# A trunk layer on one core: separate places for raw weights, low parts by adding DMAs at the channel mixer's front, and the last gate computed there

## The chip, the cores and the metric

The kernel runs on one core of a Trainium2 chip. The metric is the device time of one execution in microseconds, the median over several executions. The names of the engines are those of the profile: PE is TensorE, DVE VectorE, ACT ScalarE, POOL GpSimd, SP SyncE.

## The reference

One layer on a sequence of 512 rows of width 1024, in float32: a token mixer (attention and a diagonal state-space branch on one modulated input, merged by gates) and a SwiGLU channel mixer, each modulated by a conditioning vector through shift, scale and gate.

```python
mod = c_act @ w_ada[l] + b_ada[l]
sh_m, sc_m, g_m, sh_f, sc_f, g_f = [m[:, None, :] for m in jnp.split(mod, N_MOD, axis=-1)]
h = _normalize(x) * (1.0 + sc_m) + sh_m
y = token_mixer(h, ...)
x = _layer_norm(DEEPNORM_ALPHA * x + (1.0 + g_m) * y, ln1_g[l], ln1_b[l])
h = _normalize(x) * (1.0 + sc_f) + sh_f
gate, up = jnp.split(h @ w_ffn_in, 2, axis=-1)
y = (jax.nn.silu(gate) * up) @ w_ffn_out
x = _layer_norm(DEEPNORM_ALPHA * x + (1.0 + g_f) * y, ln2_g[l], ln2_b[l])
```

`w_in` has 4096 columns (q, k, v, the state-space input u and two gates of 1024), `w_ffn_in` 2 x 2816, `w_ada` 6 x 1024.

## The kernel before

Every large product runs on PE in three matmuls on rounded operands (`mm3`): high times high, high times low, low times high. So each weight tile of 128x1024 passes four steps: SP loads it into a raw place, ACT casts it to its high part `whi` (L178, L1054), and the low part `wlo` is raw minus high. `unit` has two ways for the low part: a subtraction on DVE or POOL (`sub`, recorded as L159), or, with `eng=None`, ACT writes minus raw (L180) and a DMA from POOL's queue adds raw to it (L181). `whi` and `wlo` have four places each (`NHI`); `slot_unit` and `split` put such parts into the 53 general slots `s0` to `s52` instead.

**Raw places.** All raw data rotate through eight places of one tag, "raw" (`NRAW`): weights, the raw blocks of `w_ada` (`ra`), and the coefficient tables `ce` of the state-space slices (L598 to L601, two for a slice, alive from the memset on POOL to the slice's last matmul). The ninth tile of the tag waits until the first is free, the tenth for the second, whatever they hold. SP issues its loads in program order (`load`, L146), so a load that waits for its place holds back all loads behind it.

**Token mixer.** Four state-space slices (`ssm_slice`) alternate with eight dense tiles of `w_in`: six for q and k (`qk_tile`) and two for v (`v_tiles`, 256 columns, two raw pieces of 512 KB each). The gates of the conditioning vector for the token mixer and the vectors of the channel mixer's modulation are summed on DVE from `ra` blocks (`ada_acc`, L250 and L252) while gate tiles, attention and the up-projections run. Then follow the output projection (`proj`) and, block by block of 128 rows, the first layer norm (`ln1_block`, L934 to L984), which transposes on PE (L967), modulates on DVE and ACT (L972, L974) and writes high and low parts of the channel mixer's input `h` (L978, L159).

**Channel mixer, front.** Four first weights of `w_ffn_in` (two by `unit`, two by `slot_unit`; the subtraction on POOL, POOL, POOL and DVE by `FENG`), then `first_half(0)`, which multiplies them with the first 256 rows; then for the first two of ten column groups `p_x1` (product `X`) and `p_b`, each of one raw piece (`piece`) whose low part DVE subtracts in `operand` (L1054 and L159); then `first_half(256)` and `combine`.

**Channel mixer, loop.** For each of the ten groups `dp` seven products on raw pieces and their sums (`plus`, L1047). In groups 2 to 5 the loop also computes a quarter of the last gate `g_f` on PE (`ada_gate_pe`, L259 to L273: a memset on POOL, L264, one small load of `b_ada`, two loads of `w_ada` of 512 KB, 16 matmul records of 128x32 by 32x256), and in group 6 two products with `ones` spread it over the rows, into the slots `gmx` of the first gate. Then follows the down projection on `w_ffn_out`.

The order of the work on each engine is set by the framework's scheduler from the program's order, its priorities (`prio`) and the pools.

Of the kernel before, what the change touches and what calls it, by code (L numbers as in the profile page):

```python
# [13 lines left out]
F32 = mybir.dt.float32  # L14
F32R = mybir.dt.float32r
I32 = mybir.dt.int32
AF = mybir.ActivationFunctionType
ALU = mybir.AluOpType

P = 128  # L20
# [36 lines left out]
PL = 5  # L57
TAIL = 256

ENG, FENG = "VGVVVGVGGGGVVGGG", "GGGV"  # L60


XE, BE, ME, HE = "VVVV", "VVVV", "VVAVAAAV", "VVVVVVVV"
# [18 lines left out]
def _build(tc, I, out):  # L82
# [6 lines left out]
    def nm(s):  # L89
        cnt[0] += 1  # L90
        return f"{s}_{cnt[0]}"
# [50 lines left out]

    banks = [psp.tile([P, 512], F32, tag=f"b{i}", name=f"b{i}") for i in range(8)]

    def load(o, i):
        return tc.keep_in_program_order(nc.sync.dma_start(out=o, in_=i))  # L146

# [10 lines left out]
    def sub(dst, a, b, eng=V):  # L158
        return eng.tensor_tensor(dst, a, b, ALU.subtract)  # L159

    def split(x, n=512, eng=V, keep=False):

        h, l = get(F32R), get(F32R)
        acopy(h[:, :n], x[:, :n])  # L164
        sub(l[:, :n], x[:, :n], h[:, :n], eng)
        if not keep:
            put(x)
        return h, l

    def unit(view, a, b, eng=V):  # L170


        with prio("feed"):
            raw = wp.tile([P, D], F32, tag="raw", name=nm("raw"), bufs=NRAW)
            load(raw.rearrange("p (a b) -> p a b", a=a), view)
            hi = wp.tile([P, D], F32R, tag="whi", name=nm("whi"), bufs=NHI)
            lo = wp.tile([P, D], F32R, tag="wlo", name=nm("wlo"), bufs=NHI)
            acopy(hi, raw)  # L178
            if eng is None:
                act(lo, raw, AF.Copy, scale=-1.0)  # L180
                G.dma_start(out=lo, in_=raw, accum_op=ALU.add)  # L181
            else:
                sub(lo, raw, hi, eng)
        return hi.rearrange("p (a b) -> p a b", a=a), lo.rearrange("p (a b) -> p a b", a=a)

    def slot_unit(view, a, b, eng=V):

        raw = wp.tile([P, D], F32, tag="raw", name=nm("raw"), bufs=NRAW)
        load(raw.rearrange("p (a b) -> p a b", a=a), view)
        return [split(raw[:, h * 512:(h + 1) * 512], 512, eng, keep=True) for h in range(2)]  # L190

# [49 lines left out]
    def ada_acc(dst, src, n, init=None):  # L241

        m = D // n
        for k in range(KC):
            if k % m == 0:
                raw = wp.tile([P, D], F32, tag="raw", name=nm("ra"), bufs=NRAW).rearrange("p (k n) -> p k n", k=m)
                load(raw, src[:, k:k + m, :])
            r_ = raw[:, k % m, :]
            if k == 0 and init is None:
                ts(dst, r_, ca[:, 0:1], None, ALU.mult)  # L250
            else:
                stt(dst, r_, ca[:, k:k + 1], init if k == 0 else dst, ALU.mult, ALU.add)  # L252
# [8 lines left out]
    def ada_gate_pe(j, i, dst):  # L261

        col = j * D + i * 256
        G.memset(dst, 0.0)  # L264
        load(dst[0:1, :], I["b_ada"][0:1, col:col + 256])
        o = bk.get()
        for k0 in (0, 4):
            raw = wp.tile([P, D], F32, tag="raw", name=nm("ra"), bufs=NRAW).rearrange("p (k n) -> p k n", k=4)
            load(raw, w_ada[:, k0:k0 + 4, col:col + 256])
            for g in range(4):  # L270
                mm(o[32 * g:32 * g + 32, 0:256], caz[:, k0 + g, :], raw[:, g, :], k0 == 0, k0 == 4, tile_position=(0, 32 * g))
        tt(dst, o[:, 0:256], dst, ALU.add)
        bk.put(o)  # L273

# [291 lines left out]
    def ssm_slice(s):  # L566
# [29 lines left out]
        shc = [P, 4, 5, 16]  # L596
        ce = []
        for i in range(2):  # L598
            x_ = wp.tile([P, D], F32, tag="raw", name=nm("ce"), bufs=NRAW)[:, 0:640]
            G.memset(x_, 0.0)  # L600
            ce.append(x_.rearrange("p (q l g c) -> p q l g c", q=4, l=5, g=2))  # L601
        l5 = [bc(x[:, q4, 0:5], shc, [3]) for x in (lre, lim, nre, nim)]
# [109 lines left out]
    for s in range(4):  # L712
        with prio("ssm"):
            ys.append(ssm_slice(s))
        with prio("qkv"):
            for f in dense[2 * s:2 * s + 2]:
                f()
    put(spar_, *sbc_, *spp)


    HALVES = [(0, [(384, [(0, 0, 256), (1, 256, 128)])]),
# [181 lines left out]
    with prio("mix"):  # L903
# [92 lines left out]
        for i in range(NT):  # L996
            with prio("first"):
                ln1_block(i)
        put(*l1g, *l1b)


    with prio("ffn"):
        first, wx = [], []
        for i in range(FIRST):
            for c in (0, FH):
                view = w_f[:, :, c + P * i:c + P * i + P]
                if len(first) < 2:
                    w = unit(view, KC, P, (V, G)[FENG[len(first)] == "G"])
                    w = [[x[:, k, :] for x in w] for k in range(KC)]
                else:  # L1010
                    pair = slot_unit(view, KC, P, (V, G)[FENG[len(first)] == "G"])
                    wx += pair
                    w = [[x[:, k % 4 * P:k % 4 * P + P] for x in pair[k // 4]] for k in range(KC)]
                first.append(w)
        part = [get() for _ in range(FIRST)]

        def first_half(n0):
            ts_ = slice(n0, n0 + 256)
# [17 lines left out]

        def piece(dp, c, k0):
            with prio("feed"):
                raw = wp.tile([P, D], F32, tag="raw", name=nm("raw"), bufs=NRAW)
                col = c + P * (FIRST + 2 * dp)  # L1040
                load(raw.rearrange("p (a b) -> p a b", a=4), w_f[:, k0:k0 + 4, col:col + 256])
            return raw

        def plus(x, y):
            with prio("feed"):
                r = wp.tile([P, D], F32, tag="raw", name=nm("raw"), bufs=NRAW)
                tt(r, x, y, ALU.add)  # L1047
            return r

        def operand(x):  # L1050
            with prio("feed"):
                hi = wp.tile([P, D], F32R, tag="whi", name=nm("whi"), bufs=NHI)
                lo = wp.tile([P, D], F32R, tag="wlo", name=nm("wlo"), bufs=NHI)
                acopy(hi, x)  # L1054
                sub(lo, x, hi)
            return hi, lo

        def product(o, x, h, first):
            w = operand(x)
            for q in range(2):  # L1060
                for k in range(4):
                    cs = slice(k * 256 + q * P, k * 256 + q * P + P)
                    mm3(o[:, q * 256:q * 256 + 256], [x_[:, cs] for x_ in w], h[k], first and q == 0 and k == 0, k == 3)
# [39 lines left out]
        def p_x1(dp):  # L1103
            d = dps[dp]
            d["a"], d["c"] = piece(dp, 0, 0), None
            d["X"], d["c1"] = bk.get(), get()
            product(d["X"], d["a"], half(0, 0), True)
            acopy(d["c1"], d["X"])

        def p_b(dp):  # L1110
            d = dps[dp]
            d["b"] = piece(dp, 0, 4)
            o = bk.get()
            product(o, d["b"], half(4, 0), True)
            tt(d["c1"], o, d["c1"], ALU.add)
            bk.put(o)
            silu(d["c1"])

        first_half(0)
        for dp in range(2):  # L1120
            p_x1(dp)
# [4 lines left out]
        for x in wx:  # L1126
            put(*x)
        acts, spent = [], []
        gfx = gmx
        for g in part:  # L1130
            h_ = split(g)
            acts.append(lambda m, h_=h_: [x[:, m * P:(m + 1) * P] for x in h_])
# [1 line left out]
        for dp in range(ND):  # L1134
            d, nxt = dps[dp], 2 <= dp + 1 < ND
            c_, d_ = piece(dp, FH, 0), piece(dp, FH, 4)
            s1 = plus(c_, d_)
            s2 = plus(s1, d["a"])
            product(d["X"], s2, hM, False)
            v = get()  # L1140
            acopy(v, d["X"])
            y = bk.get()
            product(y, s1, hN, True)
            product(d["X"], plus(d["a"], c_), hB, False)
            w = get()
            acopy(w, d["X"])
            tt(w, y, w, ALU.add)
            if nxt:
                p_x1(dp + 1)
            product(d["X"], d_, hD, False)  # L1150
            stt(d["c1"], d["X"], -1.0, d["c1"], ALU.mult, ALU.mult)
            bk.put(d["X"])
            if nxt:
                p_b(dp + 1)
            product(y, plus(s2, d["b"]), half(4, 256), False)
            tt(v, y, v, ALU.add)
            bk.put(y)
            silu(v)
            stt(v, w, -1.0, v, ALU.mult, ALU.mult)
            put(w)  # L1160
            d["f"] = d["c1"], v
            if 2 <= dp < 6:
                j = dp - 2
                ada_gate_pe(5, j, gfx[j // 2][:, j % 2 * 256:j % 2 * 256 + 256])
            if dp == 6:
                for j in range(2):
                    p_ = bk.get()
                    mm(p_, ones, gfx[j], True, True)
                    act(gfx[j], p_, AF.Identity, bias=one_c)
                    bk.put(p_)  # L1170
        put(*held)
        def parts(dp):

# [5 lines left out]
        with after(silus[-1:]):  # L1179
            for m in range(NT):  # L1180
                for h in range(2):
                    act(x1[m][h], x1[m][h], AF.Copy, scale=ALPHA)
        pf = [[bk.get(), bk.get()] for i in range(NT)]
        for kc in range(NF - LAST):
            if kc == len(acts):
# [107 lines left out]
```

## Time and profile before

| | |
|---|---|
| median of 3 executions | 824.61 us (824.35 to 826.85) |
| the profiled execution | 824.6 us |
| its span, first to last instruction | 822.9 us |
| granted TensorE clock, mean over the span | 0.968 of full speed |
| DMA | 111.49 MB, 135 GB/s on average |

The span is the time between the first and the last instruction of the trace; 1.7 us of the execution lie outside it. Times on the trace count from the start of the span. PEclk is the clock granted to TensorE as a share of 2.4 GHz; half of it is 1.2 GHz. A row of a timeline gives start, duration, engine, line, operation, output<-input, and in brackets how long the engine was idle before it and what ended that.

### The profile page before, as it was taken

The page shows a single profiled execution, that of the slowest core. Times are in us where ns is not written, and L with a number is a line of the kernel's source. Part 1 is how long each engine was busy: PE and PEld are TensorE (multiplying, and loading weights), DVE is VectorE, ACT ScalarE, POOL GpSimd, SP SyncE. Part 2 cuts the span into 40 slices and gives each one's busy share as a digit, 9 for nine tenths or more (in the row PEclk, how much of TensorE's full clock was granted, in tenths as well). Part 3 has the DMA queues.
Part 4 walks back from the last instruction along what each step waited for, and adds up shares of the span by engine and source line. Part 5 has one row for each costly group of instructions (what it writes and reads, how often), then busy time and mean ns, then how long its engine had stood idle before and what let it go on. Part 6 is the DMA issues. An engine that isn't in the chain of part 4 may idle for free.

```text
span 822.9 us, 12321 instructions
## 1 busy us (share of the span) xinstructions
PE 758.1 (92%) x4767; PEld 667.5 (81%) x4767; DVE 586.4 (71%) x975; ACT 438.8 (53%) x715; POOL 148.4 (18%) x161
## 2 busy tenths in 40 slices
PE   4989989999996797999994999999999999999995
PEld 2878879988885676787883989999999999888884
DVE  5798474884658774878799898777787876434267
ACT  4375644678987676761435473534445456532211
POOL 1443244512323221001634000000000000000013
PEclk9999998999997999899998899999999999999998
DMA  9992227964207792925941004414445344440001
GB/s 281 361 242 67 52 64 153 237 137 77 52 10 196 228 232 92 350 70 187 358 120 52 1 19 136 155 53 146 144 143 183 104 139 145 157 148 27 1 26 76
DMA packets 99498, 111.49 MB, mean 135 GB/s; under 512 B 4456, under 2 KB 86384, under 8 KB 99440
## 3 DMA queue, kind: packets, MB, share of 16 engines
q1 hardware_dynamic: 95552, 96.82, 37.1%
q0 software_dynamic: 3744, 13.63, 9.0%
q8 instruction: 37, 0.61, 0.3%
q10 hardware_dynamic: 144, 0.26, 0.1%
q14 instruction: 21, 0.17, 0.1%
HBM read 94.97 MB, written 2.10 MB: 118 GB/s over the span
## 4 chain that ended last, share of the span: by engine, by line
PE 75%; DVE 10%; DMA 6%; issue 3%; ACT 2%; SPq 2%; POOL 1%; POOLq 0%; DVEq 0%; ACTq 0%
PE b L149 74%; DMA ra<-w_ada 3%; SPq L146 2%; DMA s<-w_in 1%; DVE s L252 1%; DVE st L288 1%; DMA raw<-w_glu 1%; DMA wlo<-raw 1%; DVE h L159 1%; DVE s L407 1%; DMA s<-x 0%; DVE s L159 0%; DVE s L972 0%; DVE s L943 0%; DVE s L477 0%
## 5 line engine op out<-in xcount | busy, mean ns | idle before, releaser
L149 PE MATMUL b<-h,whi 128*128 128x256 f32 (+1 forms) x896 | 216.5, 331 | 20.8 <-DVE h L159 9.4
L149 PEld LDWEIGHTS b<-h,whi 128*128 128x128 f32 x896 | 151.5, 191 | 36.5 <-DVE h L159 9.6
L159 DVE TENSOR_TENSOR wlo<-raw,whi 128x1024 fp32r<-128x1024 f32 x103 | 129.6, 1264 | 72.1 <-ACT whi L178 37.1
L149 PE MATMUL b<-s,whi 128*128 128x256 f32 (+1 forms) x800 | 168.5, 308 | 7.6 <-ACT whi L178 6.8
L149 PE MATMUL b<-h,wlo 128*128 128x256 f32 (+1 forms) x448 | 148.2, 331 | 1.4 <-DMA wlo<-raw 1.4
L149 PEld LDWEIGHTS b<-s,whi 128*128 128x128 f32 x800 | 129.7, 190 | 18.0 <-ACT whi L178 6.9
L149 PE MATMUL b<-whi,s 128*128 128x512 f32 (+1 forms) x392 | 122.6, 390 | 0.0
L149 PE MATMUL b<-s,wlo 128*128 128x256 f32 (+1 forms) x400 | 121.5, 306 | 0.0
L159 DVE TENSOR_TENSOR s<-s,s 128x512 fp32r<-128x512 f32 (+4 forms) x112 | 76.4, 689 | 56.4 <-PE b L149 23.0
L178 ACT CAST whi<-raw 128x1024 fp32r<-128x1024 f32 x66 | 69.0, 1048 | 84.7 <-PE b L149 66.5
L1054 ACT CAST whi<-raw 128x1024 fp32r<-128x1024 f32 x70 | 72.7, 1050 | 77.5 <-PE b L149 41.6
L149 PEld LDWEIGHTS b<-h,wlo 128*128 128x128 f32 x448 | 85.8, 192 | 8.9 <-DMA wlo<-raw 1.9
L149 PEld LDWEIGHTS b<-whi,s 128*128 128x128 f32 x392 | 73.2, 188 | 16.6
L149 PE MATMUL b<-s,s 128*128 128x128 f32 (+2 forms) x438 | 81.9, 317 | 2.0 <-POOL s L159 1.4
L164 ACT CAST s<-s 128x512 fp32r<-128x512 f32 (+1 forms) x106 | 57.7, 569 | 41.3 <-DMA s<-w_in 12.1
L149 PEld LDWEIGHTS b<-s,wlo 128*128 128x128 f32 x400 | 75.7, 190 | 3.7
L149 PEld LDWEIGHTS b<-s,s 128*128 128x128 f32 x438 | 68.5, 192 | 11.2 <-POOL s L159 1.6
L149 PE MATMUL b<-wlo,s 128*128 128x512 f32 (+1 forms) x196 | 76.4, 390 | 0.0
L1233 POOL TENSOR_TENSOR s<-s,s 128x512 f32<-128x512 f32 x6 | 8.5, 1430 | 357.1 <-DVE s L1232 357.1
L159 POOL TENSOR_TENSOR s<-s,s 128x512 fp32r<-128x512 f32 (+1 forms) x32 | 40.2, 1264 | 79.0 <-ACT s L164 77.6
L1047 DVE TENSOR_TENSOR raw<-raw,raw 128x1024 f32<-128x1024 f32 x40 | 48.6, 1219 | 4.8 <-DMA raw<-w_ffn_in 4.3
L252 DVE SCALAR_TENSOR_TENSOR s<-ra,ca,s 128x256 f32<-128x256 f32 x88 | 47.2, 557 | 4.0 <-DMA ra<-w_ada 3.2
(246 smaller groups left out, 1096.1 us busy)
## 6 DMA issues: line engine op xcount, KB each, us to landing
raw<-w_ffn_in SPq DMA_DIRECT2D x44, 512.0 KB, 4.5
ra<-w_ada SPq DMA_DIRECT2D x32, 512.0 KB, 7.2
raw<-w_in SPq DMA_DIRECT2D x26, 512.0 KB, 4.7
wlo<-raw POOLq DMA_DIRECT2D x26, 512.0 KB, 5.2
raw<-w_ffn_out SPq DMA_DIRECT2D x22, 512.0 KB, 3.3
wa<-w_ada SPq DMA_DIRECT2D x12, 512.0 KB, 7.6
raw<-w_out SPq DMA_DIRECT2D x12, 512.0 KB, 6.5
s<-x SPq DMA_DIRECT2D x16, 256.0 KB, 3.4
```

The costliest lines, as they stand in the source:

```text
L146: return tc.keep_in_program_order(nc.sync.dma_start(out=o, in_=i))
L149: return nc.tensor.matmul(o, lhsT, rhs, start=start, stop=stop, skip_group_check=True, **kw)
L159: return eng.tensor_tensor(dst, a, b, ALU.subtract)
L164: acopy(h[:, :n], x[:, :n])
L178: acopy(hi, raw)
L252: stt(dst, r_, ca[:, k:k + 1], init if k == 0 else dst, ALU.mult, ALU.add)
L288: V.bn_stats(st[:, i, :], x)
L407: e.scalar_tensor_tensor(p_, n, -c, p_, ALU.mult, ALU.add)
L1047: tt(r, x, y, ALU.add)
L1054: acopy(hi, x)
L1233: G.tensor_tensor(z[h], z[h], l2b[h], ALU.add)
```

## The change

Three parts, and what the scheduler makes of them.

- **Places.** The eight raw places get names, `raw0` to `raw7`. Weights rotate through 0 to 3, `ra` blocks through 4 and 5, `ce` tables through 6 and 7; after the last slice 6 and 7 join the weights. From the channel mixer's pieces on, a list of free places takes the place of rotation: 4, 5, then the weights' six; `raw_get` takes the first free one, `raw_put` gives it back after the last use.
- **Low parts by DMA.** `lower` holds both ways of making a low part. With `eng=None` the four first weights and the four products `p_x1` and `p_b` of groups 0 and 1 now take ACT and a DMA from POOL's queue. That is ten more negations on ACT (six of 128x1024, four of 128x512) and ten more adding DMAs; two subtractions of 128x1024 and two of 128x512 leave POOL, four of 128x1024 and two of 128x512 leave DVE.
- **The last gate.** The four `ada_gate_pe` and the two products with `ones` move from the loop to a place ahead of `first_half(0)`, into two new slots instead of `gmx`.

```diff
+    pieces_of = {"w": deque(range(4)), "ra": deque([4, 5]), "ce": deque([6, 7])}
+
+    def piece_of(kind, name):
+
+        i = pieces_of[kind][0]
+        pieces_of[kind].rotate(-1)
+        return wp.tile([P, D], F32, tag=f"raw{i}", name=nm(name), bufs=1)
+
+    held_raw = {}
+
+    def raw_get():
+
+        i = raws.popleft()
+        x = wp.tile([P, D], F32, tag=f"raw{i}", name=nm("raw"), bufs=1)
+        held_raw[id(x)] = i, x
+        return x
+
+    def raw_put(*xs):
+        for x in xs:
+            raws.append(held_raw.pop(id(x))[0])
...
+    def lower(l, x, h, eng):
+
+        if eng is None:
+            act(l, x, AF.Copy, scale=-1.0)
+            G.dma_start(out=l, in_=x, accum_op=ALU.add)
+        else:
+            sub(l, x, h, eng)
...
     def unit(view, a, b, eng=V):
...
-            raw = wp.tile([P, D], F32, tag="raw", name=nm("raw"), bufs=NRAW)
+            raw = piece_of("w", "raw")
...
             if k % m == 0:
-                raw = wp.tile([P, D], F32, tag="raw", name=nm("ra"), bufs=NRAW).rearrange("p (k n) -> p k n", k=m)
+                raw = piece_of("ra", "ra").rearrange("p (k n) -> p k n", k=m)
                 load(raw, src[:, k:k + m, :])
...
         for i in range(2):
-            x_ = wp.tile([P, D], F32, tag="raw", name=nm("ce"), bufs=NRAW)[:, 0:640]
+            x_ = piece_of("ce", "ce")[:, 0:640]
             G.memset(x_, 0.0)
...
     put(spar_, *sbc_, *spp)
+    pieces_of["w"].extend([6, 7])
...
-                    w = unit(view, KC, P, (V, G)[FENG[len(first)] == "G"])
+                    w = unit(view, KC, P, None)
...
-                    pair = slot_unit(view, KC, P, (V, G)[FENG[len(first)] == "G"])
+                    pair = slot_unit(view, KC, P, None)
...
         part = [get() for _ in range(FIRST)]
+        raws = deque([4, 5, *pieces_of["w"]])
...
-            product(d["X"], d["a"], half(0, 0), True)
+            product(d["X"], d["a"], half(0, 0), True, None if dp < 2 else V)
...
-            product(o, d["b"], half(4, 0), True)
+            product(o, d["b"], half(4, 0), True, None if dp < 2 else V)
...
+        gfx = [get(), get()]
+        for j in range(4):
+            ada_gate_pe(5, j, gfx[j // 2][:, j % 2 * 256:j % 2 * 256 + 256])
+        for j in range(2):
+            p_ = bk.get()
+            mm(p_, ones, gfx[j], True, True)
+            act(gfx[j], p_, AF.Identity, bias=one_c)
+            bk.put(p_)
         first_half(0)
...
-        gfx = gmx
...
-            product(d["X"], plus(d["a"], c_), hB, False)
+            raw_put(s1)
+            s3 = plus(d["a"], c_)
+            raw_put(d["a"], c_)
+            product(d["X"], s3, hB, False)
+            raw_put(s3)
...
-            if 2 <= dp < 6:
-                j = dp - 2
-                ada_gate_pe(5, j, gfx[j // 2][:, j % 2 * 256:j % 2 * 256 + 256])
```

In the order of the instructions two places change. **At the v tiles** (`v_tiles`, raw_260 and raw_263 with whi_261 and whi_264 are the two pieces of the first; ce_179 and ce_180 the tables of the second slice, ce_243 and ce_244 of the fourth), POOL before:

```order
L563 TENSOR_TENSOR ce_179_1098<-s4_181_1102,s6_182_1103 64x20x16
L560 TENSOR_TENSOR s44_183_1108<-s0_101_666,s10_11_86 128x320
L561 TENSOR_TENSOR s7_184_1109<-s0_101_666,s10_11_86 128x320
L562 TENSOR_TENSOR ce_180_1100<-s44_183_1108,s7_184_1109 64x20x16
L563 TENSOR_TENSOR ce_180_1100<-s44_183_1108,s7_184_1109 64x20x16
L574 MEMSET s14_202_1247 128x512
L574 MEMSET s15_203_1248 128x512
L181 DMA wlo_262_1552<-raw_260_1549 128x1024
L181 DMA wlo_265_1559<-raw_263_1556 128x1024
```

and with the change:

```order
L186 DMA wlo_233_1401<-raw_231_1398 128x1024
L186 DMA wlo_262_1552<-raw_260_1549 128x1024
L645 MEMSET s34_187_1126 128x512
L186 DMA wlo_265_1559<-raw_263_1556 128x1024
L586 TENSOR_TENSOR s4_181_1102<-s41_100_665,s10_11_86 128x320
L587 TENSOR_TENSOR s6_182_1103<-s41_100_665,s10_11_86 128x320
L186 DMA wlo_268_1666<-raw_266_1663 128x1024
L626 MEMSET ce_179_1098 128x640
L586 TENSOR_TENSOR s44_183_1108<-s0_101_666,s10_11_86 128x320
L626 MEMSET ce_180_1100 128x640
L587 TENSOR_TENSOR s7_184_1109<-s0_101_666,s10_11_86 128x320
L588 TENSOR_TENSOR ce_179_1098<-s4_181_1102,s6_182_1103 64x20x16
```

The adding DMAs of the v pieces (L186 now) have moved ahead of the second slice's tables, and the memsets of these tables (L626), which stood far ahead, stand right before their products. PE there, before:

```order
L149 MATMUL b4_70<-ce_179_1098,s23_185_1114 128x128
L149 MATMUL b4_70<-ce_180_1100,s16_186_1115 128x128
L149 MATMUL b4_70<-ce_179_1098,s23_185_1114 128x128
L149 MATMUL b4_70<-ce_180_1100,s16_186_1115 128x128
L149 MATMUL b7_73<-whi_261_1551,h0_64 128x256
L149 MATMUL b6_72<-whi_261_1551,h0_64 128x256
L583 MATMUL b3_69<-ident_99,s15_203_1248 128x128 x4
L590 MATMUL b4_70<-ident_99,s3_136_861 128x128 x4
L149 MATMUL b7_73<-wlo_262_1552,h0_64 128x256
```

and with the change:

```order
L170 MATMUL b6_72<-h1_65,whi_232_1400 128x512
L170 MATMUL b6_72<-h0_64,wlo_233_1401 128x512
L170 MATMUL b7_73<-whi_261_1551,h0_64 128x256
L170 MATMUL b7_73<-wlo_262_1552,h0_64 128x256
L170 MATMUL b7_73<-whi_261_1551,h1_65 128x256
L170 MATMUL b7_73<-whi_261_1551,h0_64 128x256
L170 MATMUL b7_73<-wlo_262_1552,h0_64 128x256
```

The first v tile's matmuls came after the slice's matmuls on ce_179 and around its successor's transposes; now they follow the last matmul on wlo_233, and the slice's come some thirty rows later.

**At the channel mixer's front** SP before (raw_712 and raw_717 are the third and fourth first weight, raw_724 the piece of `p_x1` of group 0, raw_728 that of group 1):

```order
L146 DMA raw_712_4295<-w_ffn_in 128x8x128
L146 DMA raw_717_4305<-w_ffn_in 128x8x128
L146 DMA raw_724_4417<-w_ffn_in 128x4x256
L146 DMA raw_728_4449<-w_ffn_in 128x4x256
L146 DMA raw_732_4481<-w_ffn_in 128x4x256
```

and with the change (raw_734 and raw_738 are these two pieces, raw_726 to raw_733 the eight blocks of the last gate):

```order
L167 DMA raw_727_4333<-w_ada 128x4x256
L167 DMA s28_724_4323<-b_ada 1x256
L167 DMA raw_728_4342<-w_ada 128x4x256
L167 DMA raw_729_4348<-w_ada 128x4x256
L167 DMA s3_725_4324<-b_ada 1x256
L167 DMA raw_730_4357<-w_ada 128x4x256
L167 DMA raw_731_4363<-w_ada 128x4x256
L167 DMA s3_725_4324<-b_ada 1x256
L167 DMA raw_732_4372<-w_ada 128x4x256
L167 DMA raw_733_4378<-w_ada 128x4x256
L167 DMA raw_734_4489<-w_ffn_in 128x4x256
L167 DMA raw_738_4522<-w_ffn_in 128x4x256
```

The pieces' loads now stand behind eight loads of `w_ada` and four of `b_ada`. PE there, before (whi_707 is the first weight's high part, s30_713 the first half of the third's, L967 the transposes of the layer norm):

```order
L967 MATMUL b3_69<-ident_99,s33_689_4169 128x128 x4
L967 MATMUL b2_68<-ident_99,s52_688_4157 128x128 x4
L149 MATMUL b7_73<-h0_64,whi_707_4285 128x256
L149 MATMUL b0_66<-h0_64,s30_713_4297 128x256
L149 MATMUL b7_73<-h1_65,whi_707_4285 128x256
L149 MATMUL b7_73<-h0_64,wlo_708_4286 128x256
```

and with the change (whi_736 and wlo_737 are the parts of raw_734, whi_740 of raw_738):

```order
L170 MATMUL b7_73<-raw_727_4333,caz_113 32x256 x3
L170 MATMUL b0_66<-raw_728_4342,caz_113 32x256 x4
L170 MATMUL b0_66<-raw_729_4348,caz_113 32x256 x4
L170 MATMUL b1_67<-s28_724_4323,ones_104 128x512
L170 MATMUL b7_73<-h0_64,whi_736_4492 128x256
L170 MATMUL b7_73<-h1_65,whi_736_4492 128x256
L170 MATMUL b0_66<-h0_64,whi_740_4525 128x256
L170 MATMUL b0_66<-h1_65,whi_740_4525 128x256
L994 MATMUL b4_70<-ident_99,s39_696_4208 128x128 x4
L994 MATMUL b5_71<-ident_99,s42_697_4220 128x128 x4
L170 MATMUL b7_73<-h0_64,wlo_737_4493 128x256
```

`first_half(0)` has moved from the first place after the transposes to behind the gate's matmuls and the products of `p_x1` and of the first `p_b`.

## Rows read from the trace of the kernel before

**Rows 1.** The page's part 1: busy time of each engine, share, instructions.

```profile
PE 758.1 (92%) x4767; PEld 667.5 (81%) x4767; DVE 586.4 (71%) x975; ACT 438.8 (53%) x715; POOL 148.4 (18%) x161
```

**Rows 2.** PE's waits: engine, line, waited for, us, times, longest.

```profile
PE b L149 <- DVE h L159: 12.0, 4, 9.4
```

**Rows 3.** Timeline of SP: the issues of weight loads, 64 to 115 us.

```profile
64.43 0.37 SPq L146 DMA_DIRECT2D raw<-w_in  x1
114.67 0.92 SPq L146 DMA_DIRECT2D raw<-w_in  x2
```

**Rows 4.** Timeline of POOL, 93 to 124 us.

```profile
96.33 0.63 POOL L600 MEMSET ce<- 128x640 f32 x1 [2.06 <-DMA wlo<-raw]
...
117.19 0.87 POOL L563 TENSOR_TENSOR ce<-s,s 64x320 f32<-64x320 f32 x1
...
120.84 0.88 POOL L181 DMA_DIRECT2D wlo<-raw  x1 [1.73 <-ACT wlo L180]
122.73 0.86 POOL L181 DMA_DIRECT2D wlo<-raw  x1 [1.01 <-ACT wlo L180]
```

**Rows 5.** Timeline of PE, 122 to 126 us.

```profile
122.92 0.63 PE L583 MATMUL b<-ident,s 128*128 128x128 f32 x4 [2.71 <-DVE s L563]
124.08 0.66 PE L590 MATMUL b<-ident,s 128*128 128x128 f32 x4 [0.54 <-ACT s L623]
125.47 0.58 PE L149 MATMUL b<-wlo,h 128*128 128x256 f32 x1 [0.74 <-DMA wlo<-raw]
```

**Rows 6.** Windows: us; busy of PE, PEld, DVE, ACT, POOL; PEclk, DMA share, GB/s.

```profile
124.50:131.50 7.00, 6.26 (x32) 6.03 (x29) 6.39 (x14) 0.00 (x0) 0.00 (x0) 0.51 0.91 213
...
445.00:460.00 15.00, 5.68 (x29) 5.68 (x30) 15.00 (x26) 1.93 (x4) 1.13 (x4) 0.54 0.00 0
```

**Rows 7.** Line L181, the adding DMAs: ns of an issue (min/median/max); us to landing.

```profile
L181 POOL DMA_DIRECT2D wlo<-raw x26: 827/869/1057, 50.9 to 303.6; - x26
...
DMA to landing us min/median/max: 4.5/5.2/8.9
```

**Rows 8.** The `ra` blocks between 240 and 330 us: ns of one multiply-add; us to landing.

```profile
L252 DVE SCALAR_TENSOR_TENSOR s<-ra,ca,s x53: 470/481/1717, 248.6 to 313.9; 128x256 f32<-128x256 f32 x53
...
DMA to landing us min/median/max: 3.6/6.7/10.6
```

**Rows 9.** Timeline of DVE, 439 to 454 us.

```profile
439.17 2.68 DVE L159 TENSOR_TENSOR h<-s,h 128x512 fp32r<-128x512 f32 x1
441.77 1.75 DVE L948 SCALAR_TENSOR_TENSOR s<-s,s 128x512 f32<-128x512 f32 x1
...
449.44 0.68 DVE L948 SCALAR_TENSOR_TENSOR s<-s,s 128x512 f32<-128x512 f32 x1
450.04 1.22 DVE L159 TENSOR_TENSOR wlo<-raw,whi 128x1024 fp32r<-128x1024 f32 x1
...
453.58 1.29 DVE L159 TENSOR_TENSOR h<-s,h 128x512 fp32r<-128x512 f32 x2
```

**Rows 10.** Timelines of POOL, ACT and SP in the same place.

```profile
438.91 2.39 POOL L159 TENSOR_TENSOR wlo<-raw,whi 128x1024 fp32r<-128x1024 f32 x1 [0.55 <-ACT whi L178]
...
437.80 1.04 ACT L178 CAST whi<-raw 128x1024 fp32r<-128x1024 f32 x1
...
411.34 0.37 SPq L146 DMA_DIRECT2D raw<-w_ffn_in  x1
```

**Rows 11.** DMA issues of the page: KB each, median us to landing.

```profile
raw<-w_ffn_in SPq DMA_DIRECT2D x44, 512.0 KB, 4.5
```

**Rows 12.** Timeline of PE: the front's start, the loop's start, the last gate.

```profile
454.32 0.58 PE L149 MATMUL b<-h,whi 128*128 128x256 f32 x1 [9.44 <-DVE h L159]
...
495.01 0.28 PE L149 MATMUL b<-s,whi 128*128 128x256 f32 x1
...
550.13 1.07 PE L149 MATMUL b<-ra,caz 128*32 128x256 f32 x16
...
620.73 1.88 PE L149 MATMUL b<-s,ones 128*128 128x512 f32 x4
```

More of the change, by code (lines that the diff above doesn't have):

```diff
@@ L58 @@
 TAIL = 256
-ENG, FENG = "VGVVVGVGGGGVVGGG", "GGGV"
+ENG = "VGVVVGVGGGGVVGGG"
 XE, BE, ME, HE = "VVVV", "VVVV", "VVAVAAAV", "VVVVVVVV"
@@ L164, in split @@
         acopy(h[:, :n], x[:, :n])
-        sub(l[:, :n], x[:, :n], h[:, :n], eng)
+        lower(l[:, :n], x[:, :n], h[:, :n], eng)
         if not keep:
@@ L178, in unit @@
             acopy(hi, raw)
[L179 to L183, printed above, removed]
+            lower(lo, raw, hi, eng)
         return hi.rearrange("p (a b) -> p a b", a=a), lo.rearrange("p (a b) -> p a b", a=a)
     def slot_unit(view, a, b, eng=V):
-        raw = wp.tile([P, D], F32, tag="raw", name=nm("raw"), bufs=NRAW)
+        raw = piece_of("w", "raw")
         load(raw.rearrange("p (a b) -> p a b", a=a), view)
@@ L267, in ada_gate_pe @@
         for k0 in (0, 4):
-            raw = wp.tile([P, D], F32, tag="raw", name=nm("ra"), bufs=NRAW).rearrange("p (k n) -> p k n", k=4)
+            r_ = raw_get()
+            raw = r_.rearrange("p (k n) -> p k n", k=4)
             load(raw, w_ada[:, k0:k0 + 4, col:col + 256])
@@ L271, in ada_gate_pe @@
                 mm(o[32 * g:32 * g + 32, 0:256], caz[:, k0 + g, :], raw[:, g, :], k0 == 0, k0 == 4, tile_position=(0, 32 * g))
+            raw_put(r_)
         tt(dst, o[:, 0:256], dst, ALU.add)
@@ L998, in _build @@
                 ln1_block(i)
-        put(*l1g, *l1b)
+        put(*l1g, *l1b, *gmx)
     with prio("ffn"):
@@ L1038, in piece @@
             with prio("feed"):
-                raw = wp.tile([P, D], F32, tag="raw", name=nm("raw"), bufs=NRAW)
+                raw = raw_get()
                 col = c + P * (FIRST + 2 * dp)
@@ L1045, in plus, with operand @@
             with prio("feed"):
-                r = wp.tile([P, D], F32, tag="raw", name=nm("raw"), bufs=NRAW)
+                r = raw_get()
                 tt(r, x, y, ALU.add)
             return r
-        def operand(x):
+        def operand(x, eng=V):
             with prio("feed"):
@@ L1054, in operand, with product @@
                 acopy(hi, x)
-                sub(lo, x, hi)
+                lower(lo, x, hi, eng)
             return hi, lo
-        def product(o, x, h, first):
-            w = operand(x)
+        def product(o, x, h, first, eng=V):
+            w = operand(x, eng)
             for q in range(2):
@@ L1150, in _build @@
             product(d["X"], d_, hD, False)
+            raw_put(d_)
             stt(d["c1"], d["X"], -1.0, d["c1"], ALU.mult, ALU.mult)
@@ L1154, in _build @@
                 p_b(dp + 1)
-            product(y, plus(s2, d["b"]), half(4, 256), False)
+            s4 = plus(s2, d["b"])
+            raw_put(s2, d["b"])
+            product(y, s4, half(4, 256), False)
+            raw_put(s4)
             tt(v, y, v, ALU.add)
@@ L1161, in _build @@
             d["f"] = d["c1"], v
-            if 2 <= dp < 6:
-                j = dp - 2
-                ada_gate_pe(5, j, gfx[j // 2][:, j % 2 * 256:j % 2 * 256 + 256])
[L1165 to L1170, printed above, removed]
         put(*held)
@@ L1182, in _build @@
                     act(x1[m][h], x1[m][h], AF.Copy, scale=ALPHA)
+        pieces_of["w"] = raws
         pf = [[bk.get(), bk.get()] for i in range(NT)]
```

## The prediction

> **What bounds the kernel now.** I read the page's busy shares first: PE is busy for 758.1 us, 92% of the span, and no other engine for more than 71% [rows 1]. So the time is PE's work plus the places where PE waits or runs at half clock, and a change counts only there. PE's waits name them; the largest entry is 12.0 us behind the DVE's low part of `h`, 9.4 of it in one piece [rows 2]. Then I read the timelines of every engine around two places that the change touches, the first v tile (about 125 us) and the channel mixer's front (about 445 us), and the windows there for the clock. PE is the engine to watch in both: in the first it was idle three times [rows 5], in the second it started 9.44 us late [rows 12], and after both it ran at 0.51 to 0.54 of full speed [rows 6].
>
> **Part 1: the places, at the v tile.** Before, SP issues a weight load at 64.43 us and the next, those of the first v tile, at 114.67, when the first slice's tables give their places back [rows 3]. That makes the adding DMAs as late as 120.84 and 122.73 [rows 4]; PE, with nothing dense to run, is idle for 2.71, 0.54 and 0.74 us, the last released by such a DMA [rows 5], together 4.0 us, and then runs for 7.0 us at clock 0.51, of which 6.26 are busy [rows 6]. At full clock that work would have taken 6.26 x 0.51 = 3.2 us, so 3.1 are lost. Now weights have their own four places, the v pieces need places that weights have long left, and they can be loaded some 50 us earlier; in the new order PE runs the v tile at once, ahead of the second slice's products. What can go is 4.0 + 3.1 = 7.1 us.
>
> What is late next: tables have only two places, so the second slice's memsets come after the first slice's last matmul, about 114.7 [rows 3]. Before, its tables were done at 117.19 + 0.87 = 118.1, with the memsets made well ahead (the last at 96.33, 0.63 us each) [rows 4]. With two of these in the way they are done at about 118.1 + 1.3 = 119.4. In the new order some thirty dense matmuls stand between the last of the earlier weight and the first product on the new tables, so that wait is covered; without the cover it costs 1.3 us. Bounds: nothing gained, or 7.1. I take 7.1: of the three releasers of rows 5 one is such a DMA, and the other two belong to the slice's own chain, beside which the v tile's dense work can now lie.
>
> **Part 2: the conditioning blocks, 240 to 330 us.** `ra` blocks have two places where eight were shared, so a load of a block waits until DVE has used the block two before, and the weights stand behind it on SP's queue. Four multiply-adds of 0.48 us use up a block, 1.9 us, and a block lands 3.6 to 10.6 us after its issue, 6.7 in the median [rows 8]. The trace of before doesn't show that wait with two places. Its price lies between a gain, if transfers that crowd each other less land like the fastest (6.7 - 3.6 = 3.1 us), and a loss of as much plus one block's use (3.1 + 1.9 = 5.0). I take 0, between the two, since no row tells which outweighs the other, and keep -3.1 and +5.0 for the range.
>
> **Part 3: the channel mixer's front.** Before, POOL's subtraction at 438.91 (2.39 us) [rows 10] lies over a DVE operation at 439.17 that takes 2.68 us, where two of its kind take 1.29 at 453.58, and the next takes 1.75 against 0.68 later [rows 9]. DVE gets back 2.0 + 1.1 = 3.1 us, and the subtractions of weights leave it too (1.22 us each for 128x1024 [rows 9]). So `h` is ready some 6 us before 454.3. But this isn't what PE waits for any more.
>
> In the new order SP loads the pieces of `p_x1` after eight blocks of the last gate, where the first piece was once issued near 411.34 [rows 10], long before it was needed. The last four blocks take the places of the four first weights, and these are free only when the adding DMA has read them. The second of these weights is cast at 437.80 in 1.04 us [rows 10]; a negation of the same shape on the same engine, by that row another 1.04, ends at 439.9; the adding DMA lands 5.2 us after its issue in the median [rows 7], at 445.1; the two weights behind it are a little later, so I put the blocks' last load at 446 and the piece's at 447. It lands 4.5 us later [rows 11], 451.5; cast and negation, 453.6; adding DMA, 458.8. PE needs that low part behind a few matmuls on the high part, so it starts in earnest at about 459 instead of 454.3: 4.7 us later. What PE did from 454.32 to the loop's start at 495.01 [rows 12], 40.7 us, it still has to do, and the gate's work on top: four groups of 16 at 1.07 and the products with `ones` at 1.88 [rows 12], 6.2 us, of which the first two groups (2.1) run while PE waits. The loop starts at 459 + 40.7 + 4.1 = 503.8, 8.8 us later than before. Then 6.2 us leave the loop, which has no idle time to hide them. Net +2.6. Ends: the landings of rows 7, 4.5 and 8.9 instead of 5.2, twice in series (from the first weights to the blocks, then to the piece), give +2.6 - 1.4 = +1.2 and +2.6 + 7.4 = +10.0; below that, a start of PE with `h` at about 448.3 gives 10.7 less, -8.1.
>
> The ten negations on ACT and ten issues on POOL (0.87 us [rows 7]) lie beside PE's wait except for those in the chain above. The loop's free list has as many places as the rotation had, and I cost it at nothing; the cover is that PE has no wait there.
>
> One rule of the Trainium skill speaks against these DMAs. DVE is busy for all of 445 to 460 us [rows 6], and 26 adding DMAs from POOL were issued in 0.83 to 1.06 us each [rows 7]. The page "SBUF — State Buffer" (section "SBUF: two separate sides", its box on DVE blocking DMA) states that a DMA from the GpSimd queue can't get its descriptors written while VectorE holds the shared port in a two-port mode. By that rule the piece's DMA would wait out DVE's operation, up to 1.22 us each time [rows 9]; the narrow spread of the 26 issues doesn't show it.
>
> **Sum.** The profiled execution took 824.6 us, which is also the median, 822.9 of them the span. 824.6 - 7.1 + 0 + 2.6 = 820.1 us.
>
> **Rivals.**
> - *A longer queue at the front (slower).* Pieces wait behind eight blocks, and these behind the adding DMAs. Against the sum: if both landings in series are like the slowest of rows 7, the front costs 10.0 and the total is 824.6 - 7.1 + 10.0 = 827.5. It ends slower than before from 7.1 - 2.6 = 4.5 us of further delay on. For it speaks that ten such DMAs and eight loads of 512 KB now share the time; against it that the transfers before it were idle there (0 GB/s from 445 to 460 [rows 6]). 0.16.
> - *The v tile gains nothing*, as the tables' wait or another takes the place of the old one: 824.6 + 2.6 = 827.2, or 823.7 with half of the gain. 0.12.
> - *The blocks of the conditioning are throttled*: 820.1 + 5.0 = 825.1. 0.08.
> - *The front gains*: the pieces come early enough and PE starts with `h`, near 448.3: 820.1 - 10.7 = 809.4, halfway 815. The program's order on SP speaks against it. 0.11.
> - *Each adding DMA waits for DVE*: ten by the 1.22 us of a subtraction [rows 9], 820.1 + 12.2 = 832.3. The issues of rows 7 speak against it. 0.03.
>
> My forecast has the remaining 0.50, with a range of its own from 816 to 824 (3 us of part 2 and the ends of part 3 near the median). The range for 8 in 10 takes in most of the rivals on either side but the 809 and the 832: 812 to 828. About 0.3%, 2.5 us, is what a measurement of this kernel can tell from no change: faster is below 822.1, slower above 827.1. Faster: most of the forecast and the gaining front, 0.56; the same: its rest, the throttled blocks and half of the v tile's case, 0.21; slower: 0.23.
>
> **What would show it.** At the v tile: loads of `w_in` right behind 64.43, no idle time of PE between 118 and 126, clock 1.00 there, and the second slice's products without a wait. In the front: no POOL subtraction, DVE's operations at 0.7 us, blocks of `w_ada` issued around 430 and again around 445, the first piece near 447, its adding DMA landing near 459, the loop's start 8.8 us later on its own scale (1.7 after the v tile's gain, near 497), and no 128x32 weights inside it. Wrong would be: PE's start in the front before 450 or after 463, idle time of PE at the tables, or new waits of PE between 244 and 330 us that add up to more than 3 us.

## The result and the profile after

The changed kernel takes 830.38 us in the median of 13 runs (827.34 to 834.66); the kernel before took 824.61 beside it. The ratio is 1.0077, 95% interval 1.006 to 1.0095: slower by 0.8%, some 6.3 us. The forecast was 820.1 with a range of 812 to 828, so it is wrong, in sign too. The profiled execution took 832.57 us, span 830.9, 2.2 us above the median; comparisons of places in the two traces carry that.

The busy times of the page hardly differ from [rows 1]: PE has the same work, and DVE less.

```profile
PE 760.4 (92%) x4767; PEld 666.8 (80%) x4767; DVE 574.8 (69%) x969; ACT 445.3 (54%) x725; POOL 147.0 (18%) x167
```

To see where the time went, I count PE's matmul records (4767 in both kernels) and compare the time on the trace at which the same number has started. The order within a stretch differs, so only the ends of a stretch say something:

| record | place | before, us | after, us | difference |
|---|---|---|---|---|
| 600 | ahead of the v tile | 105.7 | 108.4 | +2.7 |
| 800 | behind it | 139.5 | 134.7 | -4.8 |
| 1100 | last slice | 181.1 | 176.4 | -4.7 |
| 1200 | first gate tiles | 199.6 | 204.0 | +4.4 |
| 1860 | up-projections | 351.7 | 356.6 | +4.9 |
| 4766 | end | 812.9 | 820.3 | +7.5 |

Between records 600 and 800, across the v tile, 7.5 us were gained, where 7.1 were forecast. Between records 1100 and 1200, which take 18.4 us before, 9.1 us were lost, in a place that the prediction doesn't mention. The other losses are 2.7 us ahead of record 600 and 3.1 behind record 1200. PE's timeline of the changed kernel there, with columns as in [rows 5]:

```profile
192.25 0.74 PE L170 MATMUL b<-h,whi 128*128 128x512 f32 x2 [1.56 <-ACT whi L206]
195.58 0.80 PE L170 MATMUL b<-h,whi 128*128 128x512 f32 x1 [2.59 <-ACT whi L206]
197.35 0.69 PE L170 MATMUL b<-s,negtri 128*128 128x384 f32 x1 [0.55 <-ACT s L193]
200.80 0.80 PE L170 MATMUL b<-h,wlo 128*128 128x512 f32 x1 [0.63 <-DMA wlo<-raw]
```

PE waits twice for high parts of weights, once for another cast on ACT, then for a low part. The windows of that stretch, of the changed kernel and, below, of the kernel before (columns of [rows 6]):

```profile
180.00:204.00 24.00, 18.16 (x83) 14.56 (x82) 9.98 (x18) 19.51 (x33) 4.47 (x5) 0.81 0.75 178
```

```profile
180.00:204.00 24.00, 24.00 (x134) 20.79 (x133) 10.31 (x17) 19.93 (x35) 6.21 (x6) 1.00 0.38 71
```

PE was busy for all of 24 us at full clock; now it is idle for 5.8 of them, at a mean clock of 0.81. Why the weights are late stands on SP, first its timeline from 64 to 187 us of the changed kernel, then its longest wait between 100 and 260:

```profile
65.17 0.37 SPq L167 DMA_DIRECT2D raw<-w_in  x1
69.24 0.37 SPq L167 DMA_DIRECT2D raw<-w_in  x1
...
117.91 0.37 SPq L167 DMA_DIRECT2D raw<-w_in  x1
129.45 0.37 SPq L167 DMA_DIRECT2D raw<-w_in  x1
186.71 0.37 SPq L167 DMA_DIRECT2D raw<-w_in  x1
```

```profile
SPq L167 <- PE b L170: 56.8, 1, 56.8
```

The first v piece now loads at 65 us and not at 114.67 [rows 3]. But after 129.45 no weight is issued for 57 us. After the slices, `pieces_of["w"].extend([6, 7])` puts the tables' two places at the end of the weights' rotation. Four more weights take 0 to 3; the fifth and sixth get 6 and 7, where the **last** slice's tables come first and stay until that slice's last matmul on them, at 186.6. SP issues in order, so four more weights stand behind these two, all of them of the gate tiles that PE is to run next. All six are then issued within 7 us, and the first low part lands at 200.75.

### The profile page after: what moved, and what is told of

It reads as the page before. It is cut to its first block, busy times and chain, and to the rows that moved or that the text cites. A ratio compares the mean times of both kernels' runs of the same rounds, so it can differ in the third digit from the quotient of the medians.

```text
span 830.9 us, 12346 instructions
## 1 busy us (share of the span) xinstructions
PE 760.4 (92%) x4767; PEld 666.8 (80%) x4767; DVE 574.8 (69%) x969; ACT 445.3 (54%) x725; POOL 147.0 (18%) x167
## 4 chain that ended last, share of the span: by engine, by line
PE 50%; DMA 9%; DVE 4%; issue 2%; ACT 2%; SPq 0%; POOL 0%; POOLq 0%; ACTq 0%
PE b L170 49%; DMA wlo<-raw 4%; DMA raw<-w_in 2%; DMA raw<-w_out 2%; DMA s<-raw 1%; DVE st L314 1%; DMA raw<-w_ffn_in 1%; ACT whi L206 1%; ACT s L193 1%; SPq L167 0%; ACT wlo L185 0%; DVE s L276 0%; DVE mv L319 0%; DVE s L999 0%; DVE s L970 0%
## 5 line engine op out<-in xcount | busy, mean ns | idle before, releaser
L170 PE MATMUL b<-h,whi 128*128 128x256 f32 (+1 forms) x896 | 221.3, 338 | 16.8 <-ACT whi L1082 11.3
L170 PEld LDWEIGHTS b<-h,whi 128*128 128x128 f32 x896 | 154.7, 195 | 33.6 <-ACT whi L1082 12.6
L170 PE MATMUL b<-s,whi 128*128 128x256 f32 (+1 forms) x800 | 164.1, 304 | 0.0
L170 PE MATMUL b<-h,wlo 128*128 128x256 f32 (+1 forms) x448 | 151.0, 338 | 10.9 <-DMA wlo<-raw 10.9
L180 DVE TENSOR_TENSOR wlo<-raw,whi 128x1024 fp32r<-128x1024 f32 x99 | 121.1, 1232 | 50.9 <-ACT whi L206 39.7
L180 DVE TENSOR_TENSOR s<-s,s 128x512 fp32r<-128x512 f32 (+4 forms) x112 | 79.4, 717 | 53.9 <-PE b L170 27.6
```

What stands on the lines that cost most here:

```text
L170: return nc.tensor.matmul(o, lhsT, rhs, start=start, stop=stop, skip_group_check=True, **kw)
```

## The experiments

Each kernel's time is given as its ratio to the kernel before on the same chip, with the 95% interval. "Late join" is this edit, in `piece_of`: 6 and 7 join the end of the rotation when the 21st weight is drawn, not behind the tenth.

```diff
+        if kind == "w":
+            drawn.append(name)
+            if len(drawn) == 21:
+                pieces_of["w"].extend([6, 7])
         i = pieces_of[kind][0]
         pieces_of[kind].rotate(-1)
...
-    pieces_of["w"].extend([6, 7])
```

"By engines" sets the low parts of the four first weights back to POOL, POOL, POOL and DVE, and those of the pieces of `p_x1` and `p_b` to DVE; "in the loop" moves the last gate's block back to groups 2 to 6 of the loop, into `gmx`. All nine combinations that were run:

| run | join | first weights | pieces | last gate | ratio |
|---|---|---|---|---|---|
| the change | at once | DMA | DMA | front | 1.0077 (1.006 to 1.0095) |
| e2 | at once | engines | engines | loop | 1.0051 (1.0031 to 1.0071) |
| e1 | late | DMA | DMA | front | 1.0020 (1.0004 to 1.0037) |
| e4 | late | DMA | DMA | loop | 1.0044 (1.0027 to 1.0062) |
| e6 | late | engines | DMA | loop | 1.0026 (1.0012 to 1.0041) |
| e9 | late | DMA | engines | front | 1.0004 (0.9968 to 1.0041) |
| e3 | late | engines | engines | loop | 0.9949 (0.993 to 0.9968) |
| e5 | late | engines | engines | front | 0.9942 (0.9918 to 0.9967) |
| e7 | late | DMA | engines | loop | 0.9946 (0.9925 to 0.9967) |

**The join.** e1 is the change with the late join; e2 and e3 are the divided places alone, joined at once and late.

> The changed kernel, but places 6 and 7 join the weights' rotation six weights later, so that no weight waits for the last slice's tables. Theory (the loss is the load that waits from 129 to 187 us for those tables, some 9 us of stall and half clock between 176 and 204): the loads follow one another, PE has no idle time over 0.5 us between 180 and 204, and the time falls by 7 to 9 us against the changed kernel, to about 822. Rival A (the front of the channel mixer is the loss): within 2 us of the changed kernel, about 829 to 831. Rival B (four places are too few for weights, whichever come after): the stalls stay near 190 us, 827 or more.

> The kernel before with the divided places alone, joined as in the change; low parts by the engines, the last gate in the loop. Theory: minus 7.5 at the v tile, plus 9 near 190 us, the front as before: about 826 (824 to 829). Rival A (the front is the loss): the v tile's gain alone is left, about 817.

> The kernel before with the divided places and the later join. Theory: the v tile's gain is left without its price, 824.6 - 7.5 = 817 (815 to 820). Rival B (four places are too few): the stall near 190 us stays, 824 or more.

e2 came out at the upper end of what the theory gave (+4.2 us by its ratio), e3 4 us above its 817 (821.2 in the median, outside the 815 to 820), e1 5 us above its 822 (827.2). The stall is gone in both late kernels; e3's timeline of SP and its window:

```profile
128.09 0.37 SPq L172 DMA_DIRECT2D raw<-w_in  x1
142.55 0.37 SPq L172 DMA_DIRECT2D raw<-w_in  x1
```

```profile
180.00:204.00 24.00, 24.00 (x130) 20.55 (x129) 10.55 (x18) 20.83 (x36) 5.92 (x6) 1.00 0.42 87
```

So the join costs 0.0051 + 0.0051 = 1.0%, 8.4 us, with the front as before (2.3 us either way by the two intervals), and four places are enough for the weights there: rival B falls. That 8.4 is so near to 9.1 is in part chance. On the traces of e2 and e3 the late join takes away 9.1 us between records 1100 and 1200; at record 1860 6.4 are left, since e3 loses 4.0 in between, and at the end it is 10.3: e2 loses another 1.5 near 405 us and 2.4 at the front. PE's order differs in part between the two from record 1074 on, and no run tells that from the stall.

With the changed front only 0.57% (4.7 us) come back. In e1's trace PE waits 2.85 us for a low part at 473.48, and the ten microseconds behind that run at 0.72; in the changed kernel the same wait is 2.25 us, and PE stays at 1.00. This low part is used 37.0 us after the end of the output projection in both; the loop then starts 68.6 us after that end in e1 and 65.0 in the changed kernel. So the missing 3.7 us lie behind that wait, and some 3 of them are the clock. First e1, then the changed kernel:

```profile
473.48 0.58 PE L175 MATMUL b<-h,wlo 128*128 128x256 f32 x1 [2.85 <-DMA wlo<-raw]
```

```profile
474.00:484.00 10.00, 10.00 (x66) 10.00 (x65) 4.57 (x9) 5.61 (x10) 0.00 (x0) 0.72 0.14 27
```

```profile
482.54 0.39 PE L170 MATMUL b<-h,wlo 128*128 128x256 f32 x1 [2.25 <-DMA wlo<-raw]
```

```profile
483.00:493.00 10.00, 10.00 (x87) 10.00 (x86) 7.55 (x15) 6.70 (x14) 0.00 (x0) 1.00 0.21 39
```

**The front.** e4 to e7 and e9 take its parts one by one.

> The changed kernel with the later join and the last gate back in the loop; the ten adding DMAs at the front stay. Theory (the front is late because the pieces' loads stand behind the gate's eight blocks): PE starts the first products near 448 on the scale of before, some 6 us earlier than before, and the time is 811 to 815, below e3. Rival (the adding DMAs themselves make the front late): PE starts no earlier than with the subtractions, and the time is that of e3 or more, 817 to 820.

> The changed kernel with the later join and the front's low parts by POOL and DVE again; the last gate stays at the front. Theory (the gate's move pays where a place of a first weight comes free by a subtraction, since its 6.2 us of PE lie in a wait of 13 us): below e3 by 3 to 5 us, 816 to 818. Rival (the pieces behind the eight blocks are late whoever makes the low parts): e3 or more, 821 to 827.

> e4 with the four first weights' low parts by POOL and DVE again; only the four products of the pieces use adding DMAs. Theory (e4 is late because the first sum of two pieces stands on DVE ahead of the low part of h and waits for a load whose place an adding DMA of a first weight holds): DVE has no wait of 7 us at 443, and the time is that of e3 within 2 us, 819 to 823. Rival (any adding DMA at the front costs, by its negations on ACT): 824 to 828.

> The reverse of e6: only the four first weights' low parts by adding DMAs, the pieces' by DVE. Theory: the place is held as in e4, the wait of the first sum on DVE stays, and the time is near e4, 826 to 830. Rival (the pieces' DMAs are what costs): near e3, 820 to 823.

> The changed kernel with the later join, where only the four first weights use adding DMAs and DVE subtracts for the pieces; the last gate at the front. Theory (the adding DMAs of the pieces are what the front loses by; those of the first weights gain 3 to 4 us; the gate's move is worth about nothing): 817 to 821, as e5 and e7. Rival (the gate's blocks and the first weights' adding DMAs together hold the pieces back as in e1): 824 to 828.

e4 missed: 829.3 against the 811 to 815 of the theory. Its trace shows a wait on DVE that I then took for the cause: the sum of two pieces stands ahead of the low part of `h`, and waits for a load that an adding DMA held back.

```profile
450.57 1.23 DVE L1079 TENSOR_TENSOR raw<-raw,raw 128x1024 f32<-128x1024 f32 x1 [7.62 <-DMA raw<-w_ffn_in]
```

e6 and e7 were to confirm it, and both went the other way: with adding DMAs for the first weights alone (e7) the time is that of e3 (-0.03%), and with adding DMAs for the pieces alone (e6) it is 0.77% above e3; on top of the first weights' they cost 0.98% (e4 against e7). So the adding DMAs of the pieces cost without the wait on DVE, which e6 doesn't have. Whether that wait costs as well is not shown, as e7 doesn't have it at its length:

```profile
452.54 1.23 DVE L1079 TENSOR_TENSOR raw<-raw,raw 128x1024 f32<-128x1024 f32 x1 [1.24 <-DMA raw<-w_ffn_in]
```

In e4's trace 3.6 us are lost against e3 between records 2200 and 2300, where `h` is late, and 3.0 more between 2400 and 2500. The second loss is the one that e6 shows alone, a hole behind the start: PE's timeline in e6, and the windows of the same stretch in e6 and then in e3.

```profile
473.50 0.65 PE L998 MATMUL b<-ident,s 128*128 128x128 f32 x4 [1.81 <-ACT s L993]
474.43 0.50 PE L175 MATMUL b<-h,whi 128*128 128x256 f32 x2 [0.28 <-ACT whi L1086]
476.50 0.58 PE L175 MATMUL b<-h,wlo 128*128 128x256 f32 x1 [1.57 <-DMA wlo<-raw]
```

```profile
471.00:481.00 10.00, 6.34 (x33) 5.66 (x33) 3.42 (x8) 7.24 (x14) 1.71 (x2) 0.73 0.55 105
```

```profile
471.00:481.00 10.00, 8.84 (x71) 8.36 (x72) 9.31 (x17) 9.45 (x20) 0.00 (x0) 1.00 0.00 1
```

For the later pieces a place of `whi` and `wlo` comes free only when PE is through with the first weights (ACT's cast of the third piece, at 469.65 in e6 and 469.93 in e3, is released by PE). So their low part is on PE's path: a subtraction takes 1.22 us [rows 9], a negation and an adding DMA 1.05 and, in e6, 4.5. PE is idle 2.5 us longer than in e3 in these ten, and the clock falls to 0.73.

The gate's move is worth nothing with subtractions (e5 against e3: -0.07%; e5's 820.3 us miss the 816 to 818 of its theory) and costs 0.58% with the first weights' adding DMAs (e9 against e7; e9's 824.2 are its rival's). The blocks take these weights' places: PE's first low part of a piece is used 15.3 us after the end of the output projection in e5, 19.6 in e9 and 24.1 in the changed kernel. With all adding DMAs the move seems to gain 0.24% (e1 against e4), but the two intervals overlap.

**Four places for the conditioning blocks, and what follows.** e3 is 8.1 us ahead of before at record 1500 (249.8 against 257.9) and 4.1 at record 1860.

> e3, but places 6 and 7 go to the conditioning blocks instead of the weights after the slices, so these have four places and weights four up to the channel mixer. Theory (two places for the blocks cost some 4 us between 250 and 350 us, where e3 gives back half of the v tile's gain): the gain of 8 us at 250 us stays, and the time is 815 to 818. Rival (what e3 gives back there is bandwidth, not places): e3's time, 820 to 822, or more, if four places hold back the weights.

e8 (`pieces_of["ra"].extend([6, 7])` in place of the join, and `raws = deque([4, 5, 6, 7, *pieces_of["w"]])`) gave 0.9970 (0.9954 to 0.9986), 822.0 us, which is its rival's time; its interval overlaps that of e3. At record 1700 it was 3.9 us ahead of e3 (303.1 against 307.0), so two places do hold back the blocks; at record 1860 both stand at 347. In between PE waits for the first weight of the gated linear unit, 7.4 us in e8, 5.3 in e3, 6.8 before: SP loads it behind the first norm's vectors, which wait for slots until attention has ended. e10 is e7 with these vectors moved behind that unit's weights, e11 does so in e9, and e12 is e7 with them behind the up-projections' weights too:

```diff
-        l1g, l1b = bcast("ln1_g"), bcast("ln1_b")
         load(bglu, I["b_glu_t"])
...
+        l1g, l1b = bcast("ln1_g"), bcast("ln1_b")
         gmx = [get(), get()]
```

> e7 with the loads of the first layer norm's scale and shift moved behind those of the weights of the gated linear unit. Theory (in every kernel here PE waits 5 to 7 us near 330 us for these weights, whose loads stand on SP behind the norm's vectors, which wait for slots until attention ends; that wait swallows what was gained ahead of it): the wait near 330 shrinks to under 2 us and the time is 812 to 816. Rival (the weights aren't the last thing PE waits for there, the branch's own activations are): e7's time, 818 to 822.

> e10 and e9 together. Theory: the gain of e10 on top of e9, 811 to 817. Rival: e9's time.

> e7 with the loads of the first layer norm's vectors moved behind all weights of the gated linear unit and the up-projections, not only behind the former as in e10 (where they held back the up-projections' weights instead: PE waited 13.7 us at 349). Theory: no load waits on SP for slots of attention before the up-projections' weights; PE's wait near 330 us shrinks to under 2 us and the time is 812 to 816, below both kernels by more than 1%. Rival (the weights aren't what PE waits for near 330): e7's time, 818 to 822.

e10 gave 1.0154 (1.0123 to 1.0185) and e11 1.0242 (1.021 to 1.0273), both far above what they were to give: the vectors now held back the up-projections, and PE waited there, in e10 for 13.7 us. e12 gave 0.9924 (0.9892 to 0.9956), 819.41 us in the median beside 825.63 before. That is the lowest ratio of all, but not the 812 to 816 expected, and its interval and that of e7 overlap. PE's waits between 300 and 360 us in e10, and then in e12:

```profile
PE b L175 <- ACT whi L211: 13.7, 1, 13.7
PE b L175 <- DMA wlo<-raw: 3.9, 2, 2.6
```

```profile
PE b L175 <- DMA wlo<-raw: 4.4, 1, 4.4
PE b L175 <- ACT s L875: 1.7, 1, 1.7
```

The wait for these weights has gone, as expected. But a gate tile's adding DMA, issued at 305.19, now runs beside their loads and lands at 313.8, and PE waits 4.4 us for it, just ahead of the unit.

## Why the prediction was wrong

**Part 1, the places, is the step that failed.** Its gain is near: 7.1 us forecast, 7.5 measured from record 600 to 800; PE has no idle time from 120 to 140 us, the first v piece is loaded at 65.17, and the second slice's tables cause no wait. What failed is the sentence on what is late next. It named the tables behind their two places, and stopped there; what the places cost the weights that come later stood in the sum at nothing, without a reason. It should have followed the places on: which weight is the first to draw place 6, and who holds it then. The order on SP shows nothing of this, as its rows are the same in both kernels up to the channel mixer; the diff line and the count of weights do. The price is 9.1 us in the trace and 8.4 by e2 and e3. With that term the sum would have been 820.1 + 8.4 = 828.5 or 820.1 + 9.1 = 829.2, and 830.4 was measured. The agreement is closer than the account: 2.7 us ahead of record 600 belong to no term.

**Part 2** is right in the sum, by chance: +0.2 us between records 1500 and 1860, forecast 0. That two places hold back the blocks is shown (between 240 and 330 us SP waits 38.1 us for DVE's multiply-adds in the changed kernel and 11.0 before, and e8's four places gain), and e3 pays 4.0 us there, inside the -3.1 to +5.0. In the changed kernel, where the stretch starts 4.7 us late, nothing is given back. Yet the sign that was named for this part is there: PE's waits between 244 and 330 us add up to 16.5 us, 4.2 more than before. SP's wait in the changed kernel, then before:

```profile
SPq L167 <- DVE s L276: 38.1, 10, 7.1
```

```profile
SPq L146 <- DVE s L252: 11.0, 6, 2.8
```

**Part 3, the front,** is near in its sum and too early in its times. The chain is the one described: PE waits for the first piece's high part, whose load stands behind the gate's blocks. On the changed kernel's own scale the projection ends at 445.6, 5.6 us later than before (440.0).

```profile
463.71 0.58 PE L170 MATMUL b<-h,whi 128*128 128x256 f32 x1 [10.24 <-ACT whi L1082]
...
469.70 0.58 PE L170 MATMUL b<-h,wlo 128*128 128x256 f32 x1
...
510.58 0.40 PE L170 MATMUL b<-s,whi 128*128 128x256 f32 x2
```

The loop starts 510.6 - 445.6 = 65.0 us behind that end, against 495.0 - 440.0 = 55.0 before: 10.0 later, where 8.8 were forecast. From there to the last matmul it is 310.0 us instead of 318.1, 8.1 less, where 6.2 were forecast. Net +1.9, forecast +2.6. That this is so near is in part luck, and it holds behind the stall alone: with the late join the changed front costs 0.71% (e1 against e3), 5.9 us. The low part is there 5.3 us later than worked out (24.1 us behind the projection's end, not 458.8 - 440.0 = 18.8), some 4 of which come back ahead of the loop, and the loop gives 1.9 more than forecast. On the scale of before PE starts in earnest at 464.1, past the 463 that was named as a sign of being wrong. What was mis-sized is the time to the piece's load, at 456.83, or 451.2 on the scale of before, where 447 was worked out: the last adding DMA of the first weights was issued 3.5 us behind that of the second weight and landed 7.5 us after its issue, where I allowed 0.9 and 5.2.

**The rivals.** The longer queue, which I gave 0.16, was to end slower by a front that costs 4.5 us more than forecast; with +1.9 against +2.6 it costs no more, though the delay that it speaks of is there, in the 5.3 us above. The v tile's gain is not in doubt. A wait of each adding DMA for DVE is not seen in the issues: the 36 of the changed kernel took 0.85 to 1.20 us, also from 445 to 449 us, where DVE had no pause. The four issued there landed after 6.0 to 7.5 us, with the DMA engines 95% busy, and no view tells whether a wait is part of that. The Trainium skill's page "SBUF — State Buffer" (section "SBUF: two separate sides", its box on DVE blocking DMA) gives its rule for VectorE in a two-port mode. No view shows the mode of DVE's operations, so no run here tests that rule, and the prediction's 1.22 us for each DMA took a subtraction for such an operation without showing it.

```profile
L186 POOL DMA_DIRECT2D wlo<-raw x32: 850/862/1179, 53.7 to 481.0; - x32
L186 POOL DMA_DIRECT2D s<-raw x4: 852/878/1202, 431.5 to 448.7; - x4
...
DMA to landing us min/median/max: 3.4/5.8/9.0
```

**Open:** all kernels with divided places are 0.5 to 2.7 us late at record 600; in the changed kernel PE waits for DVE 1.55 us at 63.34 and 1.30 at 79.42, where it waited 0.30 at 62.31 and not at all there before. No run took that apart. And e7's profiled execution was its slowest of 12 (824.9 against a median of 819.7), from a stretch between records 1500 and 1860 that took 104.7 us, 97.9 in e3 with the same order there; why that stretch varies so much wasn't settled.

## What to carry to other kernels

When a pool of buffers is divided, write down for each named place who holds it until when, and for each later draw in the rotation which place it gets: one draw from a place that another owner still holds stops every load behind it on an in-order queue, and the order of instructions doesn't show it. A low part, or any step, that goes from an engine's 1.2 us to a DMA's 5 us of latency is free where its place and its use are far apart, and costs its latency and the clock behind the hole where its buffer comes free just before its use. A load moved out of the way of one group of loads should be followed to the group that it now stands ahead of.

## What was not expected of the hardware

A hole of 2.85 us in PE's work in e1 cost some 3 us more by the ten microseconds at a mean clock of 0.72 behind it, while one of 2.25 us in the same place of the changed kernel was followed by ten at 1.00. In the changed kernel adding DMAs landed after up to 9.0 us where loads of weights ran beside them, and after 3.4 (256 KB) to 4.5 (512 KB) at the least.
